# The low part of every second feed-forward input block: an accumulating GpSimd transfer in place of a VectorE subtraction

## The chip, the cores and the metric

The kernel runs on one core of one Trainium2 chip. The core has a matrix engine (PE in the profile), VectorE (DVE), ScalarE (ACT), GpSimd (POOL), SyncE (SP, which here only issues transfers), and 16 DMA engines shared by all queues. The metric is the device time of one execution in microseconds (us), the median over runs.

## The reference

Two layers are computed in float32 on 256 tokens of width 2048. The first has a gMLP mixer, the second an attention mixer; after the mixer each layer has a SwiGLU feed-forward of inner width 5632 and a gated per-layer embedding. The change touches the feed-forward alone:

```python
FFN_DIM = -(-8 * D_MODEL // (3 * 256)) * 256

def swiglu(h, w_in, w_out):
    g, u = jnp.split(h @ w_in, 2, axis=-1)
    return (jax.nn.silu(g) * u) @ w_out
...
        x = x + swiglu(rmsnorm(x, norm_ffn[i]), ffn_w_in[i], ffn_w_out[i])
```

`w_in` is 2048 x 11264 for each layer, `w_out` 5632 x 2048.

## The kernel before

Every matrix product is made in a reduced format (fp32r) with a correction. An operand is split into a high part, rounded to that format, and a low part, the exact rest, and three products are summed: high x high, low weight x high activation, high weight x low activation (`mm3`, L90 to L93). Activations are split once, weights as they stream in.

Weights come in blocks of 2 x 128 rows and 512 columns, 512 KB each, laid out in memory so that each partition reads one contiguous run of 4 KB. `wblock` (L109) loads one on SP into a tile `raw` (four buffers), makes the high part `wh` on ScalarE (L84) and the low part `wl` on VectorE as `raw - wh` (L85), each with four buffers. A block feeds 12 matmuls: two token tiles, two k tiles, three products. `gemm` (L144) runs a chunk of 512 columns over the inner dimension 2048 in 8 such blocks.

`ffn` (L325) goes over the 11 column chunks of `w_in` in three parts of 4, 4 and 3. For each chunk it runs a gate product (tiles `g`), applies Silu on ScalarE, runs the up product (`u`), multiplies on VectorE, transposes (`mid_T`) and splits the result into `aT`. At the end of each part it runs the output product (`fo`) with `w_out`. There are 2 layers x 11 chunks x 2 products x 8 = 352 blocks of `w_in`, and 176 of `w_out`.

The order on each engine is set by a scheduler when the program is built; within an engine instructions run in that order, each waiting for its semaphores. A tile with n buffers makes the (i + n)-th user wait for the last reader of the i-th. POOL has little to do before: reciprocal roots for the norms (`rstd`, L104), four masks, and one 256 KB load, `w`.

While the first feed-forward begins, SP also copies the attention's position bias, 4224 KB, from memory to memory (`bias_rep`, L240).

Of the kernel before, what the change touches and what calls it, by code (L numbers as in the profile page):

```python
# [9 lines left out]
F32 = mybir.dt.float32  # L10
F32R = mybir.dt.float32r
AF = mybir.ActivationFunctionType
ALU = mybir.AluOpType
# [5 lines left out]
P = 128  # L19
KD = D // P  # L20
FFN = 5632
KF = FFN // P
NC = 512
NCH = D // NC
FCH = FFN // NC
# [5 lines left out]
EPS = 1e-6  # L31
NEG = -1e30
KT = 2
RW = 528
SCALE = HD ** -0.5

# chunks of the B layer's query/gate projection: (first head, heads, width, column of head 0)
Q_CHUNKS = [(0, 3, 432, 48), (3, 4, 512, 0), (7, 3, 384, 0), (10, 3, 384, 0), (13, 3, 384, 0)]

# columns of the packed small parameters  # L40
PK_GAIN = 0
# [10 lines left out]
def trunk_kernel(ctx: ExitStack, tc: tile.TileContext, a: dict, out: bass.AP):  # L52
    nc = tc.nc
# [16 lines left out]
    x_sb = const.tile([P, TT, D], F32, name="x_sb")  # L70
    # the first activation loads its function table while the first inputs are on their way
    nc.scalar.activation(neg_half[:, 8:], neg_half[:, :8], AF.Copy)
# [8 lines left out]
    def split(hi, lo, src, scale=None):  # L81
        """hi + lo = src * scale: hi is src rounded to the fp32r format, lo the exact rest."""
        if scale is None:
            nc.scalar.activation(hi, src, AF.Copy)  # L84
            nc.vector.tensor_tensor(lo, src, f32v(hi), ALU.subtract)  # L85
        else:
            nc.scalar.activation(hi, src, AF.Copy, scale=scale)
            nc.vector.scalar_tensor_tensor(lo, src, scale, f32v(hi), op0=ALU.mult, op1=ALU.subtract)
# [9 lines left out]
    def rsqrt_mean(dst, ss, n):  # L98
        """dst = (ss / n + EPS) ** -0.5"""
        w = ss.shape[-1]  # L100
        ms = sm.tile([P, 16], F32, tag="ms", name="ms")
        pr = ss.shape[0]
        nc.vector.tensor_scalar(ms[:pr, :w], ss, 1.0 / n, EPS, op0=ALU.mult, op1=ALU.add)
        nc.gpsimd.tensor_tensor(dst, ms[:pr, :w], neg_half[:pr, :w], ALU.pow)  # L104

# [1 line left out]
    last_load = [None]  # L107

    def wblock(src, off, n):  # L109
        raw = wp.tile([P, KT * NC], F32, tag="raw", name="raw", bufs=4)  # L110
        sz = P * KT * n
        last_load[0] = nc.sync.dma_start(raw[:, :KT * n], src[off:off + sz].rearrange("(p f) -> p f", p=P))
        wh = wp.tile([P, KT * NC], F32R, tag="wh", name="wh")
        wl = wp.tile([P, KT * NC], F32R, tag="wl", name="wl")
        split(wh[:, :KT * n], wl[:, :KT * n], raw[:, :KT * n])
        return wh, wl
# [3 lines left out]

    def gemm_blocks(accs, acth, actl, src, off, n, nk):
        """one closure for each KT k tiles of a chunk whose blocks start at element off"""
        def block(b):
            wh, wl = wblock(src, off + b * P * KT * n, n)
            for t in range(TT):
                cs = slice(t * P, (t + 1) * P)
                for j in range(KT):
                    k = b * KT + j
                    mm3(accs[t][:, :n], acth[:, k, cs], actl[:, k, cs],
                        wh[:, j * n:(j + 1) * n], wl[:, j * n:(j + 1) * n],  # L130
                        start=(k == 0), stop=(k == nk - 1))
        return [lambda b=b: block(b) for b in range(nk // KT)]

    def weave(blocks, side):
        """the blocks in order, with the side steps spread between them"""
        done = 0
        for i, blk in enumerate(blocks):
            blk()
            upto = len(side) * (i + 1) // len(blocks)
            for st in side[done:upto]:  # L140
                st()
            done = upto

    def gemm(nm, acth, actl, src, off, n, nk, side=()):  # L144
        accs = gemm_acc(nm)
        weave(gemm_blocks(accs, acth, actl, src, off, n, nk), side)
        return accs
# [12 lines left out]
    def x_chunk_T(dst, which, c):  # L160
        """transposed, gained and split columns of x for the next matmul"""
        hi, lo = dst
        for kk in range(0, 4, 2):
            pt = gen_bank("xT")
            for j in range(2):
                k = c * 4 + kk + j
                for t in range(TT):
                    nc.tensor.transpose(pt[:, j * SEQ + t * P:j * SEQ + (t + 1) * P],
                                        x_sb[:, t, k * P:(k + 1) * P], ident)
            for j in range(2):  # L170
                k = c * 4 + kk + j
                split(hi[:, k, :], lo[:, k, :], pt[:, j * SEQ:(j + 1) * SEQ], gain(which, k))
# [16 lines left out]
    def mid_T(dst, k0, src):  # L189
        """[tok, 4 k tiles] f32 of one chunk (per token tile) -> split, transposed"""  # L190
        hi, lo = dst
# [11 lines left out]

    # ================= layer A: gMLP mixer =================
    hT = big_pair("h", "hA")
# [24 lines left out]
    def prepare_bias(pool, tbl, oh):  # L230
        """bias_rep[p, h, m]: the masked bias of head h at distance 255 - m, the same for each p"""
        rt = pool.tile([H, RW], F32, name="rt")
# [10 lines left out]
    with ExitStack() as actx:  # L243
# [31 lines left out]
        for c in range(NCH):  # L275
# [5 lines left out]
            with tc.issue_after(last_load[0].ins):  # L281
                nc.sync.dma_start(ws, a["wsT"][:, c * 4:(c + 1) * 4, :])
            # keep s <= t (partition s, column t)
            nc.gpsimd.affine_select(out=ws, in_=ws, pattern=[[0, 4], [1, P]], base=0,
# [39 lines left out]

    def ffn(layer, hT, ss, which_next):  # L325
        rs = finish_rstd(ss)
        win = a["ffn_w_in"][layer]
# [4 lines left out]
        for pi, part in enumerate(parts):  # L332
            aT = big_pair("big", f"aT{layer}_{pi}")
            for ci, c in enumerate(part):
                accg = gemm(f"g{c}", hT[0], hT[1], win, c * CH_D, NC, KD)
                sil = tp.tile([P, TT, NC], F32, tag="t0", name="sil")
                for t in range(TT):
                    nc.scalar.activation(sil[:, t, :], accg[t], AF.Silu, scale=rs[:, t:t + 1])
                accu = gemm(f"u{c}", hT[0], hT[1], win, (FCH + c) * CH_D, NC, KD)
                ac = tp.tile([P, TT, NC], F32, tag="t1", name="ac")  # L340
# [51 lines left out]

    # ================= shared K/V and layer B: NSA mixer =================
    with ExitStack() as bctx:
# [17 lines left out]
        def compress_steps(kv):  # L412
            """the compression MLP of the keys (kv = 0) or values (kv = 1): the 8 blocks of its first
            matrix, then the steps after it"""
            st = {}

            def part(b):
# [3 lines left out]
                wh, wl = wblock(a["cmp_w1"], (kv * 8 + b) * P * 1024, NC)  # L421
                # T holds for each l [high part | rest] of 30 columns: one pass gives both rows
                for j in range(4):
# [54 lines left out]

        # selected and window branches: k | v
        def kv_proc(br, accs):  # L480
# [25 lines left out]

        # compressed branch: k_c | v_c
        cmpT = [None, None]
# [39 lines left out]
        def attn_steps(h, qh, ql, e):  # L548
            """the steps of one head; softmax rows are ordered S1 W1 S0 W0 C1 C0 (branch, token tile)"""
            g = h // (H // G)  # L550
            st = {}

            def scores():
# [6 lines left out]
                mm3(s2[:, 16:288], q0h, q0l, KTh[:, g, :272], KTl[:, g, :272], True, True)  # L560
                # bias[p, c]: distance 128 + p - c; the keys of the compressed branch end 16 apart
                bias = at.tile([P, 416], F32, tag="bias", name="bias", bufs=3)
# [17 lines left out]
                for r, (lv, sv_, bv) in enumerate(rows):  # L580
                    # lv = -(score + bias), nmx = -max(score + bias)
                    nc.vector.tensor_tensor_reduce(out=lv, in0=sv_, in1=bv, scale=-1.0, scalar=3e38,
# [12 lines left out]
            def transposes():  # L595
# [3 lines left out]
                for b in range(2):  # L599
                    nc.tensor.transpose(pa[:, b * SEQ:b * SEQ + P], L[:, 544 + b * P:544 + (b + 1) * P], ident)  # L600
                    nc.tensor.transpose(pa[:, b * SEQ + P:(b + 1) * SEQ], L[:, b * P:(b + 1) * P], ident)
                    nc.tensor.transpose(pb[:, b * P:(b + 1) * P], L[:, 256 + b * P:256 + (b + 1) * P], ident)
                    # only the first 16 rows of these two are used
                    nc.tensor.transpose(pb[:, 384 - b * P:512 - b * P], L[:, 512 + b * 16:640 + b * 16], ident)
# [80 lines left out]
        for h0, nh, n, c0 in Q_CHUNKS:  # L685
            accs = gemm(f"q{h0}", hT[0], hT[1], a["b_w_in"], off, n, KD, side)
            off += D * n
            q_T, heads = q_proc(accs, h0, nh, n, c0)
            # steps between the blocks of the next chunk: each finds its inputs ready
            sc = [head[0] for head in heads]  # L690
# [36 lines left out]

# [1 line left out]
def _tiled(w, widths=None):  # L729
    """[K, N] -> flat: per chunk of columns, per KT k tiles, [128, KT, n]"""  # L730
    import numpy as np
# [12 lines left out]
def _buckets(dist):  # L744
    """T5 buckets of the relative positions (a table of the shapes alone)"""
    import numpy as np
# [74 lines left out]
```

## Time and profile before: the profiled execution

| What | Value |
|---|---|
| median of 2 runs | 2316.38 us (2315.3 and 2317.46) |
| span of the profiled execution, first to last instruction | 2313.6 us |
| mean granted clock of the matrix engine | 0.999 |
| bytes read from HBM, written | 434.68 MB, 6.46 MB |
| transfers on SP's queue (q1), share of the 16 engines' span | 58.9% |
| transfers on POOL's queue (q0) | 80 packets, 0.26 MB, 0.0% |

The profile gives the span of the execution it recorded and no other time for it; the runs' median lies 2.8 us above it. An engine's busy time counts the time in which any of its instructions ran; matmuls overlap, so a row says 0.39 us for one while the next starts sooner. A line number may be that of a helper: L84 and L85 are the split of every operand, and the tile names tell which.

### The profile page before, as it was taken

What the parts mean: (1) busy time and instruction counts of PE and PEld (TensorE: products, weight loads), DVE (VectorE), ACT (ScalarE), POOL (GpSimd) and SP (SyncE); (2) the same over time, 40 slices, a digit from 0 to 9 for tenths busy, and PEclk for the clock granted to TensorE, in tenths of its full rate; (3) what the DMA queues carried; (4) which work ended last, traced back from release to release, by engine and by line L of the source; (5) the groups of instructions that cost most, each with busy time, mean ns of one, the idle gap of its engine ahead of it and who ended that gap; (6) DMA issues with size and microseconds to landing.
All of it is one profiled execution on the core that took longest, in us unless ns stands there. A gap on an engine that the chain in (4) does not pass through costs nothing.

```text
span 2313.6 us, 27764 instructions
## 1 busy us (share of the span) xinstructions
PE 2293.5 (99%) x10617; PEld 1903.5 (82%) x10617; DVE 1267.5 (55%) x1587; ACT 1107.5 (48%) x1471; POOL 23.9 (1%) x26
## 2 busy tenths in 40 slices
PE   8999999999999999999999999999999999999999
PEld 6888878888888888888887998888888888888887
DVE  5565554454454545555667776545545445444654
ACT  6554454443444344455557665544434443344543
POOL 0000000000000000000000000000000000000000
PEclk9999999999999999999999999999999999999999
DMA  8665675565655665556657344565555556555564
GB/s 291 188 194 180 214 237 190 191 191 191 191 190 184 195 195 184 190 186 187 183 176 239 114 149 137 183 196 184 190 194 190 190 191 191 192 190 191 187 197 149
DMA packets 122882, 438.63 MB, mean 190 GB/s; under 512 B 13708, under 2 KB 15884, under 8 KB 122237
## 3 DMA queue, kind: packets, MB, share of 16 engines
q1 hardware_dynamic: 121372, 434.40, 58.9%
q10 hardware_dynamic: 1296, 2.20, 0.3%
q8 instruction: 83, 1.36, 0.2%
q14 instruction: 51, 0.41, 0.1%
q0 software_dynamic: 80, 0.26, 0.0%
HBM read 434.68 MB, written 6.46 MB: 191 GB/s over the span
## 4 chain that ended last, share of the span: by engine, by line
PE 96%; DMA 2%; DVE 1%; ACT 1%; issue 0%; POOL 0%; SPq 0%; DVEq 0%; ACTq 0%
PE u L91 8%; PE u L93 8%; PE u L92 8%; PE fo L91 7%; PE fo L92 7%; PE fo L93 7%; PE g L92 7%; PE g L93 7%; PE g L91 7%; PE pg L91 2%; PE pg L93 2%; PE pg L92 2%; PE bo L91 1%; PE bo L93 1%; PE bo L92 1%; PE mT L196 1%
## 5 line engine op out<-in xcount | busy, mean ns | idle before, releaser
L85 DVE TENSOR_TENSOR wl<-raw,wh 128x1024 fp32r<-128x1024 f32 (+1 forms) x808 | 980.8, 1216 | 971.7 <-ACT wh L84 971.2
L84 ACT ACTIVATE wh<-raw 128x1024 fp32r<-128x1024 f32 (+1 forms) x808 | 849.4, 1053 | 1097.7 <-PE u L93 313.0
L91 PE MATMUL g<-wh,hF0h 128*128 128x512 f32 x352 | 137.3, 390 | 1.3 <-ACT wh L84 1.3
L92 PE MATMUL g<-wl,hF0h 128*128 128x512 f32 x352 | 137.9, 392 | 0.5 <-DVE wl L85 0.5
L92 PE MATMUL g<-wl,hF1h 128*128 128x512 f32 x352 | 137.8, 392 | 0.0
L93 PE MATMUL g<-wh,hF1l 128*128 128x512 f32 x352 | 137.8, 391 | 0.0
L93 PE MATMUL g<-wh,hF0l 128*128 128x512 f32 x352 | 137.7, 391 | 0.0
L91 PE MATMUL g<-wh,hF1h 128*128 128x512 f32 x352 | 137.2, 390 | 0.0
L91 PE MATMUL u<-wh,hF0h 128*128 128x512 f32 x352 | 136.9, 389 | 0.0
L92 PE MATMUL u<-wl,hF0h 128*128 128x512 f32 x352 | 136.9, 389 | 0.0
L93 PE MATMUL u<-wh,hF0l 128*128 128x512 f32 x352 | 136.9, 389 | 0.0
L91 PE MATMUL u<-wh,hF1h 128*128 128x512 f32 x352 | 136.9, 389 | 0.0
L92 PE MATMUL u<-wl,hF1h 128*128 128x512 f32 x352 | 136.9, 389 | 0.0
L93 PE MATMUL u<-wh,hF1l 128*128 128x512 f32 x352 | 136.9, 389 | 0.0
L93 PE MATMUL fo<-wh,aT_0l 128*128 128x512 f32 x256 | 99.8, 390 | 0.0
L93 PE MATMUL fo<-wh,aT_1l 128*128 128x512 f32 x256 | 99.8, 390 | 0.0
L92 PE MATMUL fo<-wl,aT_0h 128*128 128x512 f32 x256 | 99.8, 390 | 0.0
L92 PE MATMUL fo<-wl,aT_1h 128*128 128x512 f32 x256 | 99.8, 390 | 0.0
L91 PE MATMUL fo<-wh,aT_1h 128*128 128x512 f32 x256 | 99.6, 389 | 0.0
L91 PE MATMUL fo<-wh,aT_0h 128*128 128x512 f32 x256 | 99.6, 389 | 0.0
L91 PEld LDWEIGHTS g<-wh,hF0h 128*128 128x128 f32 x352 | 66.0, 188 | 15.2 <-ACT wh L84 1.7
L92 PEld LDWEIGHTS g<-wl,hF0h 128*128 128x128 f32 x352 | 66.1, 188 | 14.3 <-DVE wl L85 1.0
(272 smaller groups left out, 4181.2 us busy)
## 6 DMA issues: line engine op xcount, KB each, us to landing
raw<-in_ffn_w_in SPq DMA_DIRECT2D x352, 512.0 KB, 3.5
raw<-in_ffn_w_out SPq DMA_DIRECT2D x176, 512.0 KB, 3.5
raw<-in_a_w_in SPq DMA_DIRECT2D x64, 512.0 KB, 4.0
raw<-in_ple_gate SPq DMA_DIRECT2D x64, 512.0 KB, 3.6
raw<-in_a_w_out SPq DMA_DIRECT2D x32, 512.0 KB, 3.6
raw<-in_b_w_out SPq DMA_DIRECT2D x32, 512.0 KB, 3.5
raw<-in_kv_w SPq DMA_DIRECT2D x24, 512.0 KB, 3.7
raw<-in_b_w_in SPq DMA_DIRECT2D x24, 384.0 KB, 3.5
```

Source lines behind the costliest of these rows:

```text
L84: nc.scalar.activation(hi, src, AF.Copy)
L85: nc.vector.tensor_tensor(lo, src, f32v(hi), ALU.subtract)
L91: nc.tensor.matmul(ps, lh, rh, start=start, stop=False)
L92: nc.tensor.matmul(ps, lh, rl, start=False, stop=False)
L93: nc.tensor.matmul(ps, ll, rh, start=False, stop=stop)
L196: nc.tensor.transpose(pt[:, j * SEQ + t * P:j * SEQ + (t + 1) * P], src[:, t, (kk + j) * P:(kk + j + 1) * P], ident)
```

## The change

In the feed-forward input product every odd block (1, 3, 5, 7 of each chunk's 8; 176 of the 352) takes another way through `wblock`. Its tiles come from a pool of their own, `fw`, three buffers each: `rawd`, `whd`, `wld`. ScalarE writes the negated high part into `wld` and the high part into `whd`; a transfer issued by GpSimd then adds `rawd` onto `wld` in SBUF, 512 KB, which leaves `raw - high`, the same low part. VectorE has no part in these blocks. Even blocks, the output product and all other products are as before. The pool is opened for the length of one `ffn` call. Comments and docstrings were also dropped, which shifts the line numbers.

```diff
-    def wblock(src, off, n):
+    def wblock(src, off, n, pool=None):
+        if pool is not None:
+            raw = pool.tile([P, KT * NC], F32, name="rawd")
+            nc.sync.dma_start(raw, src[off:off + P * KT * n].rearrange("(p f) -> p f", p=P))
+            wh = pool.tile([P, KT * NC], F32R, name="whd")
+            wl = pool.tile([P, KT * NC], F32R, name="wld")
+
+            nc.scalar.activation(wl, raw, AF.Copy, scale=-1.0)
+            nc.scalar.activation(wh, raw, AF.Copy)
+            nc.gpsimd.dma_start(wl, raw, accum_op=ALU.add)
+            return wh, wl
         raw = wp.tile([P, KT * NC], F32, tag="raw", name="raw", bufs=4)
...
-    def gemm_blocks(accs, acth, actl, src, off, n, nk):
+    def gemm_blocks(accs, acth, actl, src, off, n, nk, alt=None):
...
-            wh, wl = wblock(src, off + b * P * KT * n, n)
+            wh, wl = wblock(src, off + b * P * KT * n, n, alt if b % 2 else None)
...
-    def gemm(nm, acth, actl, src, off, n, nk, side=()):
+    def gemm(nm, acth, actl, src, off, n, nk, side=(), alt=None):
         accs = gemm_acc(nm)
-        weave(gemm_blocks(accs, acth, actl, src, off, n, nk), side)
+        weave(gemm_blocks(accs, acth, actl, src, off, n, nk, alt), side)
...
     def ffn(layer, hT, ss, which_next):
+        with tc.tile_pool(name="fw", bufs=3) as fw:
+            return ffn_in(layer, hT, ss, which_next, fw)
+
+    def ffn_in(layer, hT, ss, which_next, fw):
         rs = finish_rstd(ss)
...
-                accg = gemm(f"g{c}", hT[0], hT[1], win, c * CH_D, NC, KD)
+                accg = gemm(f"g{c}", hT[0], hT[1], win, c * CH_D, NC, KD, alt=fw)
...
-                accu = gemm(f"u{c}", hT[0], hT[1], win, (FCH + c) * CH_D, NC, KD)
+                accu = gemm(f"u{c}", hT[0], hT[1], win, (FCH + c) * CH_D, NC, KD, alt=fw)
```

The scheduler orders the changed program anew. On POOL, from the gMLP's masks to the attention layer, the 176 accumulations appear (lines with a minus are of before, those with a plus of after; `rstd` are the roots for the norms, `w` is the 256 KB load):

```order
-L284 AFFINE_SELECT ws<-ws 128x512 x4
-L410 DMA w_8275<-in_cmp_w 128x512
-L104 TENSOR_TENSOR rstd<-ms,neg_half 128x2 x3
+L295 AFFINE_SELECT ws<-ws 128x512 x4
+L104 TENSOR_TENSOR rstd<-ms,neg_half 128x2
+L118 DMA wld<-rawd 128x1024 x88
+L425 DMA w_8367<-in_cmp_w 128x512
+L104 TENSOR_TENSOR rstd<-ms,neg_half 128x2 x2
```

The first layer's 88 accumulations stand between that feed-forward's own root and the next one; the load of `w`, which stood ahead of them, now follows. In the second layer three stand ahead of its root and 85 behind it.

On SP, at the start of the first feed-forward, before (the bias copies and the first loads; a number is the tile's own):

```order
L112 DMA raw_2286<-in_ffn_w_in 128x1024
L240 DMA bias_rep_91<-d0_2101 128x8448
L112 DMA raw_2304<-in_ffn_w_in 128x1024
L112 DMA raw_2322<-in_ffn_w_in 128x1024
L112 DMA raw_2340<-in_ffn_w_in 128x1024
```

and now:

```order
L122 DMA raw_2289<-in_ffn_w_in 128x1024
L251 DMA bias_rep_91<-d0_2101 128x8448
L112 DMA rawd_2307<-in_ffn_w_in 128x1024
L122 DMA raw_2326<-in_ffn_w_in 128x1024
L112 DMA rawd_2344<-in_ffn_w_in 128x1024
```

The second block, whose load follows the bias copy, is the first changed one. Later, in the steady state of a part, SP's order is this now (numbers rise in the program's order of blocks):

```order
L122 DMA raw_3040<-in_ffn_w_in 128x1024
L112 DMA rawd_2984<-in_ffn_w_in 128x1024
L122 DMA raw_3082<-in_ffn_w_in 128x1024
L112 DMA rawd_3021<-in_ffn_w_in 128x1024
L122 DMA raw_3119<-in_ffn_w_in 128x1024
```

A changed block's load stands behind the plain load of three blocks later; before, loads stood in the program's order. PE's order of blocks is the same in both.

## The prediction

> **What bounds the kernel now.** I read the page's engine totals first, to see which engine is never free; then the windows, to see whether that holds in the stages that change and how full the transfers are there; then the waits, for what each engine's idle time hangs on; last the timeline and the landings, for the prices.
>
> The first lines of the page:
>
> ```profile
> span 2313.6 us, 27764 instructions
> PE 2293.5 (99%) x10617; PEld 1903.5 (82%) x10617; DVE 1267.5 (55%) x1587; ACT 1107.5 (48%) x1471; POOL 23.9 (1%) x26
> ```
>
> PE is busy for all but 20 us of the span, VectorE for half of it. The windows say the same of the feed-forward stages (300 to 800 is the first layer's, 1700 to 2000 a piece of the second's), and two early stretches show what the DMA engines move when they are full (columns: busy us of PE, PEld, DVE, ACT, POOL with counts, granted clock, share of the 16 DMA engines, GB/s):
>
> ```profile
> 10.00:15.00 5.00, 5.00 (x20) 4.03 (x19) 3.38 (x5) 3.82 (x6) 0.00 (x0) 1.00 0.99 377
> 25.00:30.00 5.00, 5.00 (x23) 4.13 (x22) 1.59 (x4) 1.63 (x4) 0.00 (x0) 1.00 1.01 407
> 300.00:560.00 260.00, 260.00 (x1162) 214.46 (x1161) 130.64 (x120) 111.25 (x112) 0.00 (x0) 1.00 0.61 196
> 560.00:800.00 240.00, 240.00 (x1074) 197.91 (x1073) 118.99 (x107) 101.05 (x103) 0.00 (x0) 1.00 0.59 190
> 1700.00:2000.00 300.00, 300.00 (x1339) 247.63 (x1338) 149.34 (x135) 124.82 (x125) 0.00 (x0) 1.00 0.59 191
> ```
>
> In 800 us of feed-forward PE has no idle microsecond. The DMA engines are 0.6 full at 190 GB/s, while full engines moved 377 and 407 GB/s of loads. The waits (engine, line, waited for: us, times, longest) confirm it; the last row is the DMA queue's own:
>
> ```profile
> DVE wl L85 <- ACT wh L84: 971.2, 734, 4.8
> ACT wh L84 <- PE u L93: 313.0, 199, 1.7
> ACT wh L84 <- DMA raw<-in_ffn_w_in: 4.5, 4, 1.7
> SPq L112 <- DVE wl L85: 1829.1, 778, 7.2
> ```
>
> VectorE waits for ScalarE, ScalarE for PE to free a buffer, and a load only for its own buffer: everything is ahead of PE and held back by it. ScalarE waited for feed-forward input loads 4.5 us in all. So nothing taken from VectorE can shorten the span; the question is whether what replaces it still stays ahead of PE.
>
> PE's pace, from the first and the last of 55 matmuls in the timeline (start, us, engine, line):
>
> ```profile
> 299.35 0.39 PE L91 MATMUL g<-wh,hF0h 128*128 128x512 f32 x1
> ...
> 311.59 0.39 PE L91 MATMUL g<-wh,hF0h 128*128 128x512 f32 x1
> ```
>
> 54 steps in 12.24 us are 0.2267 us each. A block is 12 matmuls, 2.72 us; a pair (one old block, one changed) is 5.44 us. There are 176 pairs, 957 us of the span.
>
> **The change part by part.** Prices come from these groups (busy us, mean ns) and landings (KB each, us from issue to landing), and from the one transfer that POOL issues:
>
> ```profile
> L85 DVE TENSOR_TENSOR wl<-raw,wh 128x1024 fp32r<-128x1024 f32 x776 | 950.1, 1225 | 961.5 <-ACT wh L84 961.0
> L84 ACT ACTIVATE wh<-raw 128x1024 fp32r<-128x1024 f32 x776 | 821.9, 1060 | 1072.6 <-PE u L93 313.0 <-PE fo L93 277.7 <-PE g L93 239.0
> L410 POOL DMA_DIRECT2D w<-in_cmp_w x1 | 0.7, 722 | 92.6 <-DMA d<-rt 92.6
> raw<-in_ffn_w_in SPq DMA_DIRECT2D x352, 512.0 KB, 3.5
> w<-in_cmp_w POOLq DMA_DIRECT2D x1, 256.0 KB, 4.9
> ```
>
> VectorE loses 176 subtractions, 176 x 1.225 = 216 us of busy time. Worth 0, since PE covers it: VectorE waits 971 us anyway.
>
> ScalarE gains 176 copies (the negated high part), 176 x 1.060 = 187 us. Per pair it then does three, 3.2 of 5.44 us; even if all 48 pairs' worth of 300 to 560 fell there, it would be busy (111 + 51) of 260 us. Cost 0, under PE. If the cover goes, ScalarE being late holds the low parts and the Silu behind it on the same queue.
>
> POOL gains 176 issues. The only row is 0.722 us for 256 KB; twice that for twice the bytes would be 1.44 us, so 0.72 to 1.44 of 5.44 us. POOL has nothing else to do in these stages, and its few reciprocal roots stand ahead of the transfers or behind ones long done. Cost 0. A transfer that waits on POOL for ScalarE holds only later transfers.
>
> SP issues the same number of loads. Their order changes: a changed block's load stands behind the plain load three blocks later, and it waits for the accumulation three changed blocks earlier instead of a subtraction. PE's order of blocks is unchanged, its matmuls too: 0.
>
> The buffers make a loop over three pairs, 16.3 us: accumulation lands, SP issues the next load into that raw (0.33), it lands (3.5), ScalarE negates it (1.06), POOL issues (0.72), it lands again. That is 5.6 us plus the landing L of an accumulation, so L up to 10.7 us costs nothing. The two rows above give 3.5 (512 KB, SP) and 4.9 (256 KB, POOL, on a crowded queue): half of the limit.
>
> The transfers are the uncertain term, since no row shows an accumulation. A pair loads 2 x 512 KB = 1,049 kB. At 377 to 407 GB/s that is 2.58 to 2.78 us of full engines, which leaves 2.66 to 2.86 us for 524 kB of accumulation. Lower end: it costs what a load of its size does, one pass, 1.29 to 1.39 us; pair 3.87 to 4.17. Upper end: reading raw, reading the low part and writing it each cost a full pass, 3.86 to 4.17 us; pair 6.44 to 6.95, that is 1.00 to 1.51 over PE's 5.44. I take two passes, because each row written needs two rows read, while a load reads one: 2.58 to 2.78, pair 5.16 to 5.56. At 407 GB/s (the stretch in which only loads ran) this is 95% of PE's time and costs 0; at 377 it would be 0.12 x 176 = 21 us.
>
> On the rate of an accumulating transfer the Trainium skill speaks in Collectives: The Full Stack, section "The bandwidth ceiling: the fold count and why AG ≠ RS ≠ AR": the addition is free, but two operands are read through one ring, so it runs at about half a copy's rate, some 16 GB/s an engine. An estimate from that page's figure is 16 engines x 16 = 256 GB/s, 2.0 us an accumulation, and the sum would come out the same, 0.
>
> The start of the first feed-forward is the one place where a load is already late. From the chain of work in order of time (start, us, what):
>
> ```profile
> 276.04 17.84 DMA raw<-in_ffn_w_in
> 293.91 1.06 ACT wh L84
> 295.00 1.24 DVE wl L85
> 296.27 0.50 PE g L92
> ```
>
> This is the second block, loaded beside the 4 MB copy of the bias; it becomes a changed block. The negated copy ends at 294.97, POOL issues until 295.7, and 3.5 to 4.9 us later, at 299.2 to 300.6, the low part is there, where PE had it at 296.27: 2.9 to 4.3 us late. I take 4, since POOL's own row is the slower. The second layer's first three accumulations stand ahead of its root on POOL and are made during the stage before: 0.
>
> Sum: 2313.6 + 4 = 2317.6 of span. The runs' median, 2316.38, lies 2.8 above the profiled span, so 2320 us.
>
> **The rivals.** Slower, by the DMA engines' throughput. If an accumulation takes more than 2.66 to 2.86 us of full engines, the transfers pass PE as the bound, and every pair pays. For it: the upper end above, and no row that excludes it. Against it: the ceiling rows leave room for two passes. At three passes it gives 1.00 to 1.51 x 176 = 176 to 266 us, 2496 to 2586. At two passes and the lower rate of a mixed stretch, 318 GB/s at a share of 0.94 (so 338 when full), the pair is 6.20 us: +134, 2454.
>
> ```profile
> 276.00:300.00 24.00, 22.15 (x100) 17.62 (x99) 11.28 (x16) 10.25 (x16) 0.71 (x1) 1.00 0.94 318
> ```
>
> The Trainium skill states the premise of this rival in DMA: Bandwidth & Descriptors, section "Issuing engines are not separate DMA queues": whoever issues, transfers run on the same 16 engines and interleave. That rule, the trace agrees: weight loads landed in 17.84 us beside the bias copy instead of 3.5.
>
> Slower, by the loop's length. If an accumulation lands later than 10.7 us, a pair takes (L + 5.6) / 3 although engines are free. For it: the landing of 17.84 us on a crowded queue; accumulations share queues that would be 95% full. Against it: 3.5 and 4.9 us elsewhere. At L = 12 it costs 0.43 x 176 = 75 us, 2395; at 17.84 it costs 2.37 x 176 = 418 us, 2738.
>
> Faster: only PE's 20 us of idle time could go, and the change touches none of it but at 293 to 296, where it adds. Nothing else in the profile speaks for it.
>
> **How the numbers follow.** Hidden or nearly (up to +46 us): 0.50. Throughput: 0.33. The loop: 0.15. Faster: 0.02. A measurement of this kernel can tell about 2% from no change, here 2363 us. The likeliest case's own range is 2314 to 2345. The whole range reaches up to the three-pass end, 2590, and so leaves out the loop's worst lengths and anything beyond three passes, about 0.15; below, 2312. Chances: faster 0.02, within 2% 0.50, slower 0.48.
>
> **What would show it.** If the sum is right: the subtraction group at 808 - 176 = 632; 176 accumulations on POOL that land in under 10.7 us; 300 to 560 still 260 us of PE with a DMA share of 0.85 to 0.97; PE waiting for an accumulation only near 296. If the throughput rival is right: shares near 1.0 in the input stages, PE idle below 90% there, its idle time put down to accumulations or to ScalarE behind late loads, while the output stages (whose blocks are unchanged) keep their pace. If the loop is right: the same idle PE, but shares well under 1 and landings above 10.7 us. The forecast is wrong if a pair takes over 5.7 us.

## The result, and the profile after

| | before | after |
|---|---|---|
| median of 2 runs, us | 2316.38 (2315.3 and 2317.46) | 2348.95 (2348.4 and 2349.51) |
| span of the profiled execution, us | 2313.6 | 2347.8 |

The ratio is 1.014 (95% interval 1.011 to 1.0169): slower by 33 us, and by 29 more than the time forecast. The first lines of the page of the changed kernel:

```profile
span 2347.8 us, 28082 instructions
PE 2313.8 (99%) x10617; PEld 1905.7 (81%) x10617; DVE 1053.8 (45%) x1411; ACT 1268.2 (54%) x1647; POOL 173.5 (7%) x202
```

The 34.2 us are in two places of this line. PE is busy 20.3 us longer with the same 10617 matmuls, and it is idle 34.0 us where it was idle 20.1. The windows of the changed kernel (columns as before: window, length, busy PE, PEld, DVE, ACT, POOL with counts, granted clock, DMA share, GB/s) separate them:

```profile
300.00:310.00 10.00, 7.10 (x21) 5.66 (x22) 2.45 (x2) 3.66 (x5) 0.84 (x1) 0.60 1.05 274
300.00:560.00 260.00, 251.74 (x1094) 204.91 (x1095) 85.50 (x81) 137.24 (x142) 27.99 (x33) 0.97 0.92 261
350.00:360.00 10.00, 7.56 (x30) 6.33 (x31) 5.11 (x6) 4.61 (x6) 0.84 (x1) 0.71 1.05 315
560.00:800.00 240.00, 240.00 (x1061) 195.42 (x1060) 78.74 (x74) 129.82 (x134) 27.17 (x32) 1.00 0.91 258
1700.00:2000.00 300.00, 300.00 (x1326) 245.10 (x1325) 110.54 (x105) 153.77 (x156) 27.16 (x32) 1.00 0.85 246
```

In the last two windows PE is never idle and its clock is full, as before, yet 240 us hold 1061 matmuls where they held 1074, and 300 us hold 1326 where they held 1339. So in the steady part something makes the matmuls themselves longer. Most of the added idle time, some 12 of the 14 us, lies before 560, with the clock down to 0.60 and 0.71 at two spots.

The transfers of the changed kernel, first the queues (packets, MB, share of the 16 engines' span), then the issues (KB each, median us to landing):

```profile
q1 hardware_dynamic: 121372, 434.40, 55.4%
q0 software_dynamic: 25424, 92.55, 20.6%
...
raw<-in_ffn_w_in SPq DMA_DIRECT2D x176, 512.0 KB, 6.2
rawd<-in_ffn_w_in SPq DMA_DIRECT2D x176, 512.0 KB, 5.5
wld<-rawd POOLq DMA_DIRECT2D x176, 512.0 KB, 7.0
```

20.6% of 2347.8 us over 176 accumulations is 2.75 us of all 16 engines each. The windows above mix the input product with the output product. Apart they read as follows, first a stretch almost all of the output product, then one of the input product alone:

```profile
565.00:585.00 20.00, 20.00 (x89) 16.48 (x88) 9.78 (x9) 8.47 (x9) 0.72 (x1) 1.00 0.61 195
625.00:645.00 20.00, 20.00 (x88) 16.24 (x87) 5.42 (x5) 11.11 (x12) 2.55 (x3) 1.00 1.02 264
```

By the share the DMA engines are full in the input product, and PE still has no idle microsecond in it from 560 on: throughput is not what costs.

Where the idle time comes from, in the waits of the changed kernel (us in total, times, longest; SPq is the queue that issues loads):

```profile
PE g L92 <- DMA wld<-rawd: 5.8, 1, 5.8
PE mT L207 <- DVE ac L357: 5.4, 1, 5.4
PE g L91 <- ACT whd L117: 2.4, 1, 2.4
```

```profile
SPq L112 <- DMA wld<-rawd: 801.8, 170, 20.7
```

```profile
ACT wld L116 <- DMA rawd<-in_ffn_w_in: 39.4, 14, 7.8
```

PE waits for an accumulation once in the whole program, and for a `whd` once, both at the start of the first feed-forward. The third wait, `mT` for `ac`, is 50 us later. The chain of work in order of time (start, us, what) ties them together:

```profile
274.63 18.86 DMA rawd<-in_ffn_w_in
293.57 1.06 ACT wld L116
...
295.22 7.64 DMA wld<-rawd
302.90 0.79 PE g L92
303.70 0.43 PE g L93
304.12 0.43 PE g L91
...
329.43 5.61 DMA wld<-rawd
335.06 12.36 DMA rawd<-in_ffn_w_in
...
349.43 1.05 ACT wh L84
...
351.64 0.76 DVE ac L357
352.44 0.69 PE mT L207 x2
```

The first changed block is loaded beside the bias copy and lands late, as the second block did before; its accumulation then lands 7.64 us after POOL took it, so PE has the low part at 302.90 where it had it at 296.27. The rows of 0.43 are matmuls a little later that start 0.43 us apart instead of 0.23: the clock has fallen during the wait. The backlog has a second bill. A load for a changed block may start only when the accumulation that reads its buffer is done; the one that starts at 335.06 then takes 12.36 us on full engines (share 1.05). ScalarE waits for it 7.8 us, with an even block's `wh` (349.43) queued behind it; behind that stands VectorE's subtraction of the even block, behind the subtraction the product `ac`, and PE's transposes wait for `ac` 5.4 us.

Which matmuls are longer shows in the up product's (tile `u`) matmuls of the changed kernel (count, then min/median/max ns, first and last start in us):

```profile
L91 PE MATMUL u<-wh,hF0h x176: 387/390/396, 324.3 to 977.0; 128*128 128x512 f32 x176
L92 PE MATMUL u<-wl,hF0h x176: 388/392/398, 324.5 to 977.2; 128*128 128x512 f32 x176
L93 PE MATMUL u<-wh,hF0l x176: 389/389/390, 324.8 to 977.4; 128*128 128x512 f32 x176
L91 PE MATMUL u<-whd,hF0h x176: 393/394/395, 327.0 to 979.7; 128*128 128x512 f32 x176
L92 PE MATMUL u<-wld,hF0h x176: 393/394/395, 327.3 to 980.0; 128*128 128x512 f32 x176
L93 PE MATMUL u<-whd,hF0l x176: 393/394/395, 327.5 to 980.2; 128*128 128x512 f32 x176
```

In the up products of both layers every matmul that reads a changed block's weights takes 393 to 395 ns. Before, the same product showed 389 throughout, here in its middle row:

```profile
L92 PE MATMUL u<-wl,hF0h x352: 389/389/389, 315.2 to 956.1; 128*128 128x512 f32 x176
```

The even blocks' own matmuls lengthen a little too (medians of 390 and 392 in two of the three rows). In the timeline the step between starts goes from 0.2267 us to 0.2333:

```profile
630.99 0.39 PE L91 MATMUL g<-whd,hF0h 128*128 128x512 f32 x1
...
633.56 0.39 PE L93 MATMUL g<-whd,hF0l 128*128 128x512 f32 x1
633.79 0.39 PE L91 MATMUL g<-wh,hF0h 128*128 128x512 f32 x1
```

From 630.99 to 633.79 are 12 steps, 2.80 us for a changed block instead of 2.72: 0.08 x 176 = 14 us. The even block behind it takes 2.74 (the next changed one starts at 636.53), which adds 3 to 4 us. Two theories stand: the accumulations slow PE as they write beside it (A), or the place of the new tiles does (B).

### The profile page after: what moved, and what is told of

It is laid out like the page before. It is cut to its first block, busy times and chain, and to the rows that moved or that the text cites. A ratio compares the mean times of both kernels' runs of the same rounds, so it can differ in the third digit from the quotient of the medians.

```text
span 2347.8 us, 28082 instructions
## 1 busy us (share of the span) xinstructions
PE 2313.8 (99%) x10617; PEld 1905.7 (81%) x10617; DVE 1053.8 (45%) x1411; ACT 1268.2 (54%) x1647; POOL 173.5 (7%) x202
## 3 DMA queue, kind: packets, MB, share of 16 engines
q0 software_dynamic: 25424, 92.55, 20.6%
## 4 chain that ended last, share of the span: by engine, by line
PE 93%; DMA 4%; ACT 1%; DVE 1%; issue 1%; POOL 0%; SPq 0%; ACTq 0%; DVEq 0%; POOLq 0%
PE u L92 8%; PE u L91 8%; PE u L93 8%; PE g L92 7%; PE g L93 7%; PE g L91 7%; PE fo L91 7%; PE fo L93 7%; PE fo L92 7%; PE pg L93 2%; PE pg L92 2%; PE pg L91 2%; DMA rawd<-in_ffn_w_in 1%; PE bo L91 1%; PE bo L93 1%; PE bo L92 1%
## 5 line engine op out<-in xcount | busy, mean ns | idle before, releaser
L85 DVE TENSOR_TENSOR wl<-raw,wh 128x1024 fp32r<-128x1024 f32 (+2 forms) x632 | 765.4, 1213 | 1182.4 <-ACT wh L84 1181.8
L84 ACT ACTIVATE wh<-raw 128x1024 fp32r<-128x1024 f32 (+2 forms) x632 | 662.4, 1050 | 735.8 <-PE fo L93 275.0
L116 ACT ACTIVATE wld<-rawd 128x1024 fp32r<-128x1024 f32 x176 | 186.5, 1060 | 252.3 <-PE u L92 109.8
L118 POOL DMA_DIRECT2D wld<-rawd x176 | 149.6, 850 | 1244.4 <-ACT wld L116 1144.7
L117 ACT ACTIVATE whd<-rawd 128x1024 fp32r<-128x1024 f32 x176 | 183.8, 1044 | 0.0
L92 PE MATMUL fo<-wl,aT_0h 128*128 128x512 f32 x256 | 99.9, 390 | 0.0
L92 PE MATMUL fo<-wl,aT_1h 128*128 128x512 f32 x256 | 99.9, 390 | 0.0
L93 PE MATMUL fo<-wh,aT_0l 128*128 128x512 f32 x256 | 99.8, 390 | 0.0
L93 PE MATMUL fo<-wh,aT_1l 128*128 128x512 f32 x256 | 99.8, 390 | 0.0
L91 PE MATMUL fo<-wh,aT_0h 128*128 128x512 f32 x256 | 99.7, 389 | 0.0
L91 PE MATMUL fo<-wh,aT_1h 128*128 128x512 f32 x256 | 99.7, 389 | 0.0
L92 PE MATMUL g<-wld,hF0h 128*128 128x512 f32 x176 | 70.5, 401 | 5.8 <-DMA wld<-rawd 5.8
L92 PE MATMUL fo<-wl,aT_2h 128*128 128x512 f32 x192 | 75.5, 393 | 0.0
L93 PE MATMUL fo<-wh,aT_2l 128*128 128x512 f32 x192 | 75.5, 393 | 0.0
L91 PE MATMUL fo<-wh,aT_2h 128*128 128x512 f32 x192 | 74.9, 390 | 0.0
L91 PE MATMUL g<-whd,hF0h 128*128 128x512 f32 x176 | 69.8, 398 | 2.4 <-ACT whd L117 2.4
L93 PE MATMUL g<-whd,hF0l 128*128 128x512 f32 x176 | 70.4, 400 | 0.0
L92 PE MATMUL g<-wl,hF0h 128*128 128x512 f32 x176 | 70.3, 399 | 0.0
L92 PE MATMUL g<-wl,hF1h 128*128 128x512 f32 x176 | 69.9, 397 | 0.0
L93 PE MATMUL g<-wh,hF0l 128*128 128x512 f32 x176 | 69.8, 396 | 0.0
L91 PE MATMUL g<-wh,hF0h 128*128 128x512 f32 x176 | 69.5, 395 | 0.0
L91 PE MATMUL g<-whd,hF1h 128*128 128x512 f32 x176 | 69.4, 395 | 0.0
```

The source lines that it names most:

```text
L91: nc.tensor.matmul(ps, lh, rh, start=start, stop=False)
L92: nc.tensor.matmul(ps, lh, rl, start=False, stop=False)
L93: nc.tensor.matmul(ps, ll, rh, start=False, stop=stop)
L116: nc.scalar.activation(wl, raw, AF.Copy, scale=-1.0)
L117: nc.scalar.activation(wh, raw, AF.Copy)
L118: nc.gpsimd.dma_start(wl, raw, accum_op=ALU.add)
```

## The experiments

Each ratio is the median against that of the kernel before on the same chip, with its 95% interval.

**The new tiles without the transfer (e1).** The odd blocks keep their own pool, but VectorE subtracts.

```diff
-            nc.scalar.activation(wl, raw, AF.Copy, scale=-1.0)
-            nc.scalar.activation(wh, raw, AF.Copy)
-            nc.gpsimd.dma_start(wl, raw, accum_op=ALU.add)
+            split(wh, wl, raw)
```

> Odd feed-forward input blocks keep their own tiles (rawd, whd, wld in the pool of three) but get their low part from VectorE again; no GpSimd transfer. In the changed kernel the matmuls that read whd and wld take 394 ns in the up product where those of before took 389. Theory A, accumulating transfers in flight slow PE's reading: here 389 ns for u<-whd, and a span of 2312 to 2318 us. Theory B, the place of the new tiles in memory slows it: u<-whd stays at 394 ns and the span is 2325 to 2332 us (2 layers x 7.7 us of lost pace over 2313.6). Both: the stalls of the changed kernel near 296 and 345 us are gone.

2331.64 us, 1.0067 (1.0052 to 1.0082), span 2331.1. With no accumulation at all the changed blocks' matmuls are as long, here in the up product:

```profile
L92 PE MATMUL u<-wld,hF0h x176: 394/394/394, 318.9 to 964.5; 128*128 128x512 f32 x176
```

PE is idle 20.9 us (2331.1 - 2310.2), as before. B holds and A falls: half of the loss has nothing to do with the transfer.

**The transfer without anyone waiting for it (e2, e3).** The kernel before, with 176 transfers of 512 KB by GpSimd into a tile that nobody reads: accumulating in e2, plain copies in e3. They come from a zeroed tile `dsrc`, and the ScalarE pass that precedes them has the size of the negation.

```diff
+        if pool is not None:
+            dum = pool.tile([P, KT * NC], F32, name="dum")
+            nc.scalar.activation(dum, f32v(wh), AF.Copy, scale=0.0)
+            nc.gpsimd.dma_start(dum, dsrc[0], accum_op=ALU.add)   # e3: without accum_op
```

> All blocks get their low part as before the change, and per odd input block ScalarE also clears a scratch tile and GpSimd accumulates a tile of zeros onto it, 512 KB, which no engine waits for. Theory A (transfers in flight slow PE): matmuls of the up product lie above 389 ns where an accumulation is in flight, PE's busy time grows by 12 to 18 us, span 2326 to 2333. Theory B (place of the tiles): 389 ns, span 2312 to 2318. Both: GpSimd's queue takes 20 to 21% of the 16 engines' span, about 2.75 us an accumulation, and PE has no stall near 345 us.

e2: 2326.64 us, 1.0043 (1.0026 to 1.006), span 2327.2. The matmuls stay at 389 ns and PE is busy 2297.8 us, only 4.3 more than before. The time lies in the range that stood beside A, but not for A's reason: most of it is lost at the start.

```profile
280.00:310.00 30.00, 25.93 (x111) 20.58 (x110) 12.99 (x16) 14.01 (x20) 3.95 (x5) 0.94 0.87 252
300.00:360.00 60.00, 56.24 (x245) 46.00 (x244) 27.20 (x25) 34.70 (x35) 9.35 (x11) 0.97 1.02 284
560.00:800.00 240.00, 240.00 (x1074) 197.90 (x1073) 120.27 (x109) 135.14 (x135) 27.18 (x32) 1.00 0.91 260
```

At full pace again from 560 (1074 matmuls), but with full DMA engines in 300 to 360, and some 4 us of PE lost in either of the two early windows, which overlap by 10 us. The first of the two is not the accumulations' doing: before loses 1.85 us there itself, and the load that PE waited for had landed at 293.4, while the first accumulation was issued at 296.73. The second is theirs, since e3, below, with plain copies in their place, loses nothing there. I had written that no stall near 345 would come without a wait on the accumulation; that was a miss. Accumulations on the crowded start are enough, waited for or not.

> As the idle accumulation, but the transfer only copies the tile of zeros onto the scratch tile: one row read for each written instead of two. If an accumulation's price on the DMA engines is two passes, as the prediction took it, GpSimd's queue takes 9 to 11% of the engines' span here, 1.3 to 1.5 us a transfer; if the price is something else of accumulation or of reading SBUF, it stays near 20%. PE: under theory A by mere reading and writing of SBUF, a loss of 6 to 9 us (half as long in flight), span 2320 to 2323; if only adding slows PE, or under theory B, span 2312 to 2318.

e3: 2315.24 us, 0.9999 (0.999 to 1.0009). The plain copies cost nothing, at the start neither. The queue rows of e2 and of e3:

```profile
q0 software_dynamic: 25424, 92.55, 20.2%
```

```profile
q0 software_dynamic: 25424, 92.55, 9.8%
```

The same packets and bytes take 20.2% of e2's span, 2.67 us each, and 9.8% of e3's, 1.29 us: adding costs twice what copying does, as with two passes against one.

**The start as before (e4).** The first chunk of the first layer goes the old way, the other 168 changed blocks the new one.

```diff
+                alt = None if layer == 0 and c == 0 else fw
-                accg = gemm(..., alt=fw)
+                accg = gemm(..., alt=alt)
...
-                accu = gemm(..., alt=fw)
+                accu = gemm(..., alt=alt)
```

> The changed kernel, but the first of the first layer's 11 column chunks (its gate and up product, 8 odd blocks) takes the old way. Theory: the start costs what is not lost pace, since the first changed block meets the 4 MB bias copy, starves PE at 296 us, and the backlog starves it again near 345 us; then both stalls go, PE's idle time falls from 34.0 to 19 to 22 us, and the span is 2327 to 2332. Rival: any start of the changed blocks after plain ones costs this; then idle time stays above 30 us, moved to the second chunk near 340 to 390 us, and the span is 2340 to 2348.

2332.05 us, 1.0072 (1.0057 to 1.0087), span 2330.6: 17 us less than the changed kernel. PE's idle time is 20.9 us again (2330.6 - 2309.7), and matmuls on changed tiles still take 394 ns. So the stall belongs to the bias copy's neighbourhood, and is not paid later by whichever chunk begins. The second layer of the changed kernel agrees: its feed-forward begins with changed blocks and no copy beside them, and PE has no idle microsecond from 1470 to 1600, though three of its accumulations were made ahead. No run moves the copy itself.

**The place of the tiles (e5, e6).** In the built programs the byte at which a tile starts within a partition is known. `wh` and `wl` start 96 bytes past a multiple of 128 (116192, for one), and so do the activations of the feed-forward products (34272); the pool `fw` puts `whd` and `wld` 32 past (189344). e5 puts 64 bytes ahead of them; e6 does so and has e4's start.

```diff
+            pad = fw.tile([P, 16], F32, name="pad", bufs=1)
+            nc.gpsimd.memset(pad, 0.0)
```

> The changed kernel with 64 bytes per partition put ahead of its new tiles, so that rawd, whd and wld start at 96 bytes past a multiple of 128, as raw, wh and wl do, instead of 32 bytes past. Theory B1, the start address within 128 bytes sets the matmul's pace: u<-whd falls from 394 to 389 ns, span 2331 to 2335 (the start's stalls stay). Theory B2, the place in the upper part of memory sets it: 394 ns, span 2345 to 2350. Rival A again (accumulations slow PE): 394 ns only while they are in flight, span above 2340.

e5: 2332.35 us, 1.0058 (1.0041 to 1.0075), span 2334.6, 13 us less than the changed kernel. The median is 389 ns:

```profile
L92 PE MATMUL u<-wld,hF0h x176: 388/389/497, 327.9 to 973.6; 128*128 128x512 f32 x176
```

The stalls at the start remain: PE is idle 35.9 us (2334.6 - 2298.7).

> Both parts undone at once: the 64 bytes, and the first of the first layer's chunks takes the old way. If start and address are all that the change costs, the span is 2311 to 2319 and the ratio to before 0.998 to 1.002, although 168 accumulations run and the DMA engines are as full as in the changed kernel. Rival: the full DMA engines cost something of their own; then 2322 or more.

e6: 2317.14 us, 1.0001 (0.9992 to 1.0011), with 168 accumulations in it.

```profile
560.00:800.00 240.00, 240.00 (x1074) 197.90 (x1074) 80.61 (x78) 131.55 (x135) 27.15 (x32) 1.00 0.91 259
```

Before's pace, with VectorE busy 80.6 us instead of 119.0 and the DMA engines at 0.91 (1.02 to 1.03 in the input product alone). The two parts are the whole loss: by spans the place is worth 13.2 (changed kernel less e5) or 13.4 (e4 less e6), the start 17.2 (less e4) or 17.4 (e5 less e6). By medians the four differences are 16.6, 14.9, 16.9 and 15.2.

**What about the place counts (e7, e8, e11, e12).** The kernel before, with nothing changed but where tiles start. In e7, e8 and e11 bytes ahead of the weight tiles shift these alone, and a second pad behind them keeps the rest in place; in e12 a pad ahead of the residual shifts weights and activations together.

```diff
+    pad = wp.tile([P, 16], F32, name="pad", bufs=1)      # e8: 8 words, e11: 24
+    nc.gpsimd.memset(pad, 0.0)
+    wq = ctx.enter_context(tc.tile_pool(name="wq", bufs=1))
+    pad2 = wq.tile([P, 16], F32, name="pad2")            # e8: 24 words, e11: 8
+    nc.gpsimd.memset(pad2, 0.0)
```

```diff
+    pad = const.tile([P, 16], F32, name="pad")           # e12
+    nc.gpsimd.memset(pad, 0.0)
```

> The kernel before with all weight tiles (raw, wh, wl) moved by 64 bytes per partition, from 96 to 32 bytes past a multiple of 128; the tiles behind them move by 128 bytes and keep their place within 128. Nothing else is changed. Theory B1: every weight matmul takes 394 instead of 389 ns, 808 blocks x 12 x 0.0066 us = 64 us, span 2370 to 2382. Theory B2: 2311 to 2317.

> The same with 32 bytes, so that the weight tiles start at a multiple of 128 (the tiles behind them move by 128). Theory B1 does not say which of the other starts is best: if 96 is one of the good ones, 2311 to 2317; if a multiple of 128 is better still, up to 6 ns a matmul less, 2255 to 2310; if only 96 is good, as for 32 bytes past, 2370 to 2382. Theory B2: 2311 to 2317.

> The kernel before with its weight tiles moved by 96 bytes per partition, to 64 past a multiple of 128. So far 96 past gave 389 ns, 32 past gave 388 to 394 in turns, a multiple of 128 gave 395. If a start off a multiple of 64 is what is good, this is like the multiple of 128: 394 to 396 ns, 2364 to 2376. If it is nearness to the end of a 128-byte line, something between: 2317 to 2364.

> The kernel before with every tile from the residual on moved by 64 bytes per partition: weights (moving operand) and activations (stationary operand) then both start at 32 bytes past a multiple of 128, where before both were at 96 past, and in the seventh run only the weights had moved. Theory C1, equal starts of the two operands are what is fast: 389 ns for all matmuls, span 2311 to 2317. Theory C2, the weight tile's own start counts: as in the seventh run, L91 394 and L92 389 ns in turns, span 2328 to 2336.

| kernel | weights start at (mod 128) | activations | median ns, `u` products L91, L92, L93 in order | us | ratio |
|---|---|---|---|---|---|
| before | 96 | 96 | 389 | 2316.38 | 1 |
| e7 | 32 | 96 | 394, 389, 392 | 2332.3 | 1.0065 (1.005 to 1.008) |
| e8 | 0 | 96 | 395, 395, 395 | 2369.41 | 1.0224 (1.0209 to 1.024) |
| e11 | 64 | 96 | 394, 399, 392 | 2368.71 | 1.0227 (1.0212 to 1.0242) |
| e12 | 32 | 32 | 389, 389, 389 | 2315.48 | 0.9998 (0.9989 to 1.0008) |

The rows of the middle product (`wl` by the high activations), first of e8, then of e12:

```profile
L97 PE MATMUL u<-wl,hF0h x352: 393/395/398, 323.0 to 980.9; 128*128 128x512 f32 x176
```

```profile
L94 PE MATMUL u<-wl,hF0h x352: 389/389/389, 313.3 to 954.0; 128*128 128x512 f32 x176
```

Start 32 is no worse than start 96 as such: with the activations at 32 too, nothing is lost. The case that e11 met, that a start off a multiple of 64 is good, does not fit e7, whose weights at 32 are off one too. What the rows go by is whether weights and activations start at the same place: the two equal pairs are fast, and the three differing ones are slower, by 15 to 53 us. Equal starts at 0 or at 64 were not run. The sum that I made for e7, 394 ns for all of them and some 64 us, was four times too much; that one of its three products stays at 389 and one at 392 explains a part of this.

e7 has the same starts modulo 128 as the changed blocks and is milder than they are (394 in all three). Modulo 256 the starts differ: 160 for the changed blocks (189344), 32 for e7's weights (116256), with the activations at 224 (34272). The equal pairs are equal modulo 512 too. So it is not shown that 128 is the length that counts, and what in the chip makes the start matter is open.

**How much room the buffers and the engines have (e9, e10).** Both start from e6. e9 has two buffers instead of three; e10 sends all 8 blocks of a chunk the new way, with four.

```diff
-        with tc.tile_pool(name="fw", bufs=3) as fw:
+        with tc.tile_pool(name="fw", bufs=2) as fw:      # e10: bufs=4
...
-            wh, wl = wblock(..., alt if b % 2 else None)
+            wh, wl = wblock(..., alt)                    # e10 alone
```

> The run that undid both parts (64 bytes, old first chunk), with two buffers in the new pool instead of three. The loop of the prediction then spans two pairs, and a pair takes (L + 5.6) / 2 with L the landing of an accumulation. With the median of the changed kernel, 7.0 us, that is 6.3 us against PE's 5.44: 0.86 x 168 = 144 us, 2440 to 2480, with the DMA share of the input stages below 0.85. Rival: the landing shrinks to the 4.7 us that was the shortest when the engines are less full, 5.15 us a pair: no cost, 2312 to 2325.

e9: 2390.72 us, 1.0311 (1.0285 to 1.0338), span 2396.3. Neither figure was met. A pair took (2396.3 - 2317.2) / 168 = 0.47 us more than e6's 5.44, so 5.91. The landings in it:

```profile
rawd<-in_ffn_w_in SPq DMA_DIRECT2D x168, 512.0 KB, 4.5
wld<-rawd POOLq DMA_DIRECT2D x168, 512.0 KB, 5.2
```

The loop over two pairs is then 0.33 + 4.5 + 1.06 + 0.85 + 5.2 = 11.94, 5.97 a pair. The formula holds with the landings that were measured; what I put into it did not, since I used landings of the fuller queues, and here they are shorter. Nor did the DMA share of the input product fall below 0.85: most stretches of 20 us show 0.86 to 0.96. With three buffers and the changed kernel's landings the loop is 0.33 + 5.5 + 1.06 + 0.85 + 7.0 = 14.7, under the 16.3 that PE takes.

> All blocks of the input product, not only the odd ones, take the accumulation (four buffers, 64 bytes, first chunk old: 336 accumulations). With 2.75 us an accumulation and 1.29 to 1.39 us a load the DMA engines need 4.04 to 4.14 us a block against PE's 2.72: 1.32 to 1.42 x 336 = 444 to 477 us, 2757 to 2795, DMA share near 1.0 in the input stages and PE busy about 66% there. Rival: an accumulation's busy share is partly waiting that overlaps other packets, and the engines do more when pressed; then below 2700.

e10: 2691.85 us, 1.1622 (1.1604 to 1.1639), span 2690.2.

```profile
640.00:800.00 160.00, 126.93 (x500) 92.90 (x501) 5.58 (x8) 84.62 (x90) 33.97 (x40) 0.97 1.04 263
```

PE is busy 79% of this stretch with the DMA engines full (1.04); over the whole program it waits 256 us for accumulations. The share alone does not say that they bound the kernel, since the changed kernel has 1.02 without a wait. 168 more blocks go this way than in e6 and each pair takes 2.22 us more ((2690.2 - 2317.2) / 168), so a block takes (5.44 + 2.22) / 2 = 3.83 us instead of 2.72. I had added a load and an accumulation to 4.04 to 4.14; the time is the rival's, in which pressed engines do somewhat more. Full engines are not the only reading: with the landings here (6.5 for a load, 8.1 for an accumulation) a loop over four buffers, made up as for e9, takes 16.8 us, 4.2 a block, so it is too long as well, and no run separates the two.

No kernel of these beats before; e3, e6 and e12 equal it.

## Why the prediction was right or wrong

The time lies within the stated range and within 2% of the time before, but 4 us above the likeliest case's own range of 2314 to 2345. That it did not come out higher is luck: the 33 us come from a term that the sum had at nothing and from one that it had four times too small, and nothing in the argument kept either of them small. A pair took 5.54 us (POOL's issues follow one another at this distance), under the 5.7 that was to show the forecast wrong.

Subtractions, 216 us off VectorE worth 0: right. The page of the changed kernel has 632 of them, and VectorE only waits longer for ScalarE:

```profile
L85 DVE TENSOR_TENSOR wl<-raw,wh 128x1024 fp32r<-128x1024 f32 (+2 forms) x632 | 765.4, 1213 | 1182.4 <-ACT wh L84 1181.8
```

ScalarE's 187 us hidden: right. It is busy 129.8 of 240 us and PE waits for none of it there. What was named as the case without cover (a late ScalarE holds what is queued behind it) did come once, at 347 to 351.

POOL at 0.72 to 1.44 us an issue: right, 0.85 (149.6 us over 176).

The loop of three buffers: right in its result, with a wrong term. A load took 5.5 us, not 3.5, so the limit on an accumulation's landing was 16.3 - 7.7 = 8.6 us, not 10.7, against a median of 7.0 (the longest was 11.0). e9 shows the loop itself.

The accumulation at two passes, 2.58 to 2.78 us: right, 2.75. Over 300 to 560 the share is 0.92, where the forecast had 0.85 to 0.97, but PE is busy 251.7 us there and not 260. In the input product alone the share is 1.02: the sign that was to mark the throughput rival came, and PE's wait did not, so the share by itself tells nothing of that rival. PE waits in e10, with two changed blocks a pair, where the loop is too long as well. The row of 17.84 us beside the bias copy does not show transfers of different issuers sharing the engines, since SP issued both; the changed kernel does, with SP's loads landing in 5.5 and 6.2 us beside POOL's accumulations instead of 3.5.

**PE's matmuls, "unchanged: 0": this step failed.** Their order and number are unchanged, their length is not: about 13 us by spans, 15 to 17 by medians. The step took the new pool as a change of names. e1 shows the cost without any transfer, and e5 and e6 take it away with 64 bytes.

**The start, +4 us: the step was mis-sized**, and measured 17 by spans, 15 to 17 by medians. Of the 17, 13 are idle time (34.0 less e4's 20.9) and 4 are busy time at the lower clock (2313.8 less 2309.7). The place and the mechanism were right: the first accumulation is late, and PE waits for it near 296. Three things were missing. The accumulation landed in 7.64 us, longer than the 4.9 taken. PE's clock fell during the wait, to 0.60 over 300 to 310. And the backlog came back at 335 to 352, through a load that had to wait for an accumulation. Only the first could have been read from the trace of before, from the landing of 17.84 us beside the same copy; that row was used for the rival of the loop, not for this landing.

The sum: 4 came out as 13 + 17, and the rest of the 34 us of span (about 4) is of the size by which e6's span, 2317.2, exceeds before's while their medians agree (ratio 1.0001). One missing part is a cost of the new tiles' place, paid in every changed block, and the other a cost of one crowded moment; the transfers, engines and buffers of the steady stage, on which most of the argument was spent, behave as worked out but for the sizes named.

## What to carry to other kernels

A change that brings new tiles is also a change of addresses: compare the duration of the same matmuls before looking for a wait, and if all are longer by a constant, move the new tiles so that they start as the old ones did. In a kernel bound by PE, work that is free in the steady state is paid where the cover is thin, so try the first blocks, those beside another large transfer, the old way. A chain load, copy, transfer, consumer takes more than its first lateness: check what it queues up for the next round of the same buffers.

## What the runs showed of the hardware

The pace of these matmuls depends on where their two operands start within a partition: 0.2267 us a step with both at 96 or both at 32 past a multiple of 128 bytes (389 ns each), up to 399 ns with different starts, 2.2 to 2.3% of the whole time in e8 and e11. The matmuls of an equal pair that follow differing ones can lengthen too (390 and 392 ns in the changed kernel).

An accumulating transfer of 512 KB from SBUF onto SBUF takes 2.67 to 2.75 us of all 16 engines, a plain one 1.29, a ratio of 2.1. The Trainium skill gives the reason for collectives in Collectives: The Full Stack, section "The bandwidth ceiling: the fold count and why AG ≠ RS ≠ AR": an add needs two source reads on the same ring, and so runs at half a copy's rate. The trace agrees with that rule, for a transfer inside one core's SBUF too; the reason itself no run here shows.

In the changed kernel, after 293.99, PE ran only two matmuls (296.36) until 302.90; its next ones started 0.43 us apart for 5 us, then 0.23 again. The Trainium skill, TensorE: Matmul & The Clock Gate, Part 1, has the clock halved after some 3.4 us without work, with starts 426.7 ns apart for 512 columns. The trace agrees with the 0.43; for the length of the slow stretch it shows 4.9 us (302.90 to 307.76). In e2 an idle stretch of 3.6 us (290.91 to 294.51) was followed by a slow one of 3.6 (294.51 to 298.07).
